# A hybrid block on one core: dumps and chunk loads moved to ScalarE's DMA queue, a third tile for each part of a weight slab, RWKV outputs in the chunks' tiles, transposes in two PSUM banks by turns

## The chip, the cores and the metric

The kernel runs on one core of a Trainium2 chip. A core has five engines with an instruction queue each, and every queue is worked off in its own order: PE (TensorE, matrix products; its weight loads are listed apart as PEld), DVE (VectorE), ACT (ScalarE), POOL (GpSimd) and SP (SyncE, which here does nothing but issue DMAs). ACT can issue DMAs too; it then does so from the same queue in which its activations, copies and casts stand. Data lies in SBUF (128 partitions) or HBM; PE writes to PSUM.

The metric is the device time of one execution in microseconds (us), lower is better.

## The reference, cut to what matters

One transformer block over 512 tokens of width 1024 in float32, with three mixers side by side:

```python
h = rms_norm(x, mix_pre_g[l])
z = h @ w_in[l]                                  # 1024 x 11200
o_hg  = hgrn2_mixer(zq, zf, zi, zog, ...)        # 8 heads, gated linear recurrence
o_rw  = rwkv7_mixer(zrw, ...)                    # 16 heads, state x decay + rank-1 updates
o_mla = mla_mixer(zcq, zckv, zkr, ...)           # 8 heads, causal softmax attention
merged = g_hg*(o_hg @ w_branch[0]) + g_rw*(o_rw @ w_branch[1]) + g_mla*(o_mla @ w_branch[2])
x = x + rms_norm(merged @ w_out[l], mix_post_g[l])
gate, up = split(rms_norm(x, ffn_pre_g[l]) @ w_ffn_in[l])
x = x + rms_norm((silu(gate) * up) @ w_ffn_out[l], ffn_post_g[l])
```

At the end of the RWKV mixer stands, for each token and head, a normalisation over 64 values, an affine (`lnx_g`, `lnx_b`), the sum with a `bonus` and the product with a gate `g`. In the kernel the bonus is kept in HBM as `bv`, the gate as `grw`, and the result as `orw`.

## The kernel before

**Dense streams.** All large products go through `slab` and `stream`. A slab is 256 rows of a weight by 256 columns (256 KB). SP loads it into `wsD` (three buffers), ACT casts it to `whD` (the high part, in PE's reduced float32 type), DVE subtracts to get `wlD` (the low part), and PE makes three products for each tile of it: high by high, high by low, low by high (`mm3`, lines 139 to 141). One slab gives 12 matmuls of 128x512; four slabs fill two PSUM banks `mmD`, which ACT or DVE empties (`zst` for the input projection and the gates, `th` for the branches, `ft` in the FFN). `whD` and `wlD` take the pool's default of two buffers each. In `project` some slabs are held, with as many buffers as are held (`hold`).

**The mixers beside them.** RWKV is prepared in four groups of four heads (`rwkv_group`). Each group fills a tile `G`; its lower-triangular parts go through HBM (`Ld`), are inverted on DVE (`inv`, lines 635 and 636), come back (`Td`) and are merged; then `G` is written to HBM, `rwd`, by four DMAs (lines 460 and 461), two of them of 2240 KB. These are the dumps. After the last group the chain (`rwkv_chain`) runs over eight chunks of 64 tokens; each chunk is loaded by four DMAs of 640 KB from `rwd` (line 682) into one of three buffers `CH`. Their memory is that of `G`, so the first of them has to wait until the last dump has landed. HGRN heads (`ph`, `hq`, `hk`) and the low-rank part of MLA are spread through the same stretch.

**The RWKV tail.** After the chain, for each of eight pieces `p`: four transposes into the PSUM bank `yb` (pool `pY`, one buffer), three activations on ACT into `lno` (two buffers), a load of `bv` into `lnx` (one buffer), an addition on DVE, a load of `grw` into the same `lnx`, a product on DVE, and the store of `orw` (lines 733 to 748). Branch 0 (HGRN's output by its weights) is streamed in the same stretch: its weights, its input `ost` and its gates `th` are loaded by SP as well.

**What sets the order.** The program is written as lanes, each with a priority, and a scheduler with a timeline of its own fixes one order for each engine when the kernel is built; a changed buffer count, queue or tile moves instructions all over the program. At run time each engine follows its list: an instruction that waits holds all that stands behind it. `pace` lets a group of three products start only when the group five before it has ended, through a small memset on POOL (`token`); that is why POOL's list is full of them. DMAs share eight completion semaphores in turn, so a DMA also waits for the one that last had its semaphore.

Of the kernel before, what the change touches and what calls it, by code (L numbers as in the profile page):

```python
# [12 lines left out]
F32R = mybir.dt.float32r  # L13
# [4 lines left out]
ALU = mybir.AluOpType  # L18
# [4 lines left out]
P = 128  # L23
S = 512
# [12 lines left out]
NC = S // C  # L37
# [5 lines left out]
RWC = 5 * P  # L43
# [61 lines left out]
class Kern:  # L105
# [92 lines left out]
    def slab(self, src, pool=None, hold=None):  # L198

        nc = self.nc  # L200
        m, n = src.shape[1:]
        st = self.t(self.wd, [P, m, n], "wsD", bufs=3)
        nc.sync.dma_start(st, src)
        h, l = (self.t(pool or self.wd, [P, m, n], t, F32R, hold) for t in ("whD", "wlD"))
        cur = self.cur_lane
        self.lane(0)
        nc.scalar.copy(h, st)  # L207
        self.split_low(l, st, h)
        self.lane(cur)
        return h, l  # L210
# [231 lines left out]
    def rwkv_group(self, g):  # L442

        all_ = self.t(self.gp, [P, 2, NC, RWC], "G", bufs=2)
        G = self.fields(all_)
        G["all"] = all_
        for e in range(2):

            self.nc.gpsimd.memset(G["PV"][e][e * 64:e * 64 + 64], 0.0)
        G["Ld"] = self.t(self.dpool, [64, 32, 32], "Ld", bufs=2)  # L450
        G["Td"] = self.t(self.dpool, [64, 32, 32], "Td", bufs=2)
        for q in range(2):
            self.lane(5)
            self.rwkv_prep(G, 2 * g + q, q)
        self.lane(3)
        self.rwkv_inverse(G, g)
        self.rwkv_merge(G, g)
        for q in range(2):
            to = self.rwd[g][:, :, q].rearrange("c p n -> p c n")
            self.nc.sync.dma_start(to[:, :NC - 1], all_[:, q, :NC - 1])  # L460
            self.nc.sync.dma_start(to[:, NC - 1, :RWC - P], all_[:, q, NC - 1, :RWC - P])

    def fields(self, t):

# [204 lines left out]
    def rwkv_chain(self):  # L669

        nc, rw = self.nc, self.rw
        V, A, Pl = nc.vector, nc.scalar, nc.gpsimd
        mm = nc.tensor.matmul
        H = [slice(0, 64), slice(64, 128)]
        heads = [(p, e) for p in range(8) for e in range(2)]
        chunks = []

        def load(c):
            t = self.t(rw, [P, 8, RWC], "CH", bufs=3)
            n = RWC if c < NC - 1 else RWC - P  # L680
            for g in range(4):
                nc.sync.dma_start(t[:, 2 * g:2 * g + 2, :n], self.rwd[g][c][:, :, :n])
            chunks.append(self.fields(t))

        load(0)
        St = self.t(rw, [P, 8, C], "St")
        y = self.t(rw, [P, NT, 8, 2, C], "y")
        for c in range(NC):
            if c < NC - 1:
                load(c + 1)  # L690
            G = chunks[c]
            X, PV, LM, BKT = (G[n] for n in ("X", "PV", "LM", "BKT"))
            if 0 < c < NC - 1:

                for e in range(2):
                    Pl.tensor_tensor(St[H[e]], PV[e][H[e]], self.gC[H[e], :, c + 1:c + 2].to_broadcast([64, 8, C]), op=ALU.mult)
            yo = (H[c % 2], H[1 - c % 2])
            z = self.t(self.pC, [P, 8, C], "zus")
            for p, e in heads:
                mm(z[H[e], p, :], lhsT=X[e][:, p, 0:C], rhs=PV[e][:, p, :], start=True, stop=True)  # L700
            zsb = self.t(rw, [P, 8, C], "zsb")
            V.tensor_copy(zsb, z)
            yb = self.t(self.pY, [P, 8, C], "yb")

            self.side_by_side(
                partial(mm, yb[yo[e], p, :], lhsT=X[e][:, p, C:], rhs=PV[e][:, p, :], start=p == 0, stop=False)
                for p, e in heads)
            z = self.t(self.pC, [P, 8, C], "zus")
            for p, e in heads:
                mm(z[H[e], p, :], lhsT=LM[H[e], p, 0:C], rhs=zsb[H[e], p, :], start=True, stop=True)  # L710
            V.tensor_copy(PV[0][H[0]], z[H[0]])
            A.copy(PV[1][H[1]], z[H[1]])
            if c < NC - 1:
                z = self.t(self.pC, [P, 8, C], "zus")
                for p, e in heads:
                    mm(z[H[e], p, :], lhsT=BKT[:, p, H[e]], rhs=PV[e][:, p, :], start=True, stop=True)
                for e in range(2):
                    nxt = chunks[c + 1]["PV"][e][H[e]]
                    if c == 0:
                        V.tensor_copy(nxt, z[H[e]])  # L720
                    else:
                        V.tensor_tensor(nxt, z[H[e]], St[H[e]], op=ALU.add)
            for p, e in heads:
                mm(yb[yo[e], p, :], lhsT=LM[H[e], p, C:], rhs=PV[e][H[e], p, :], start=False, stop=p == 7)
            for e in range(2):
                A.copy(y[yo[e], c // 2, :, e, :], yb[yo[e]])
            if c % 2:
                self.lane(3)
                self.rwkv_norm(y[:, c // 2].rearrange("t p e d -> t (p e) d"))
                self.lane(1)  # L730
        self.lane(3)
        for p in range(8):
            pt = self.t(self.pY, [P, S], "yb")
            for i in range(NT):
                nc.tensor.transpose(pt[:, i * P:(i + 1) * P], y[:, i, p].rearrange("t e d -> t (e d)"), self.ident)
            o = self.t(rw, [P, S], "lno", bufs=2)
            o4 = o.rearrange("f (i j t) -> f i j t", j=2, t=C)
            pt4 = pt.rearrange("f (i j t) -> f i j t", j=2, t=C)
            lb, lg = self.vec("rwkv_lnx_b", p), self.vec("rwkv_lnx_g", p)
            A.activation(o[H[0]], pt[H[0]], AF.Identity, bias=lb[H[0]], scale=lg[H[0]])  # L740
            for j in range(2):

                A.activation(o4[H[1], :, j, :], pt4[H[1], :, 1 - j, :], AF.Identity, bias=lb[H[1]], scale=lg[H[1]])
            for src, op in ((self.bv[p], ALU.add), (self.grw[p], ALU.mult)):
                x = self.t(rw, [P, S], "lnx")
                nc.sync.dma_start(x, src)
                V.tensor_tensor(o, o, x, op=op)  # L747
            nc.sync.dma_start(self.orw[p], o)
            self.dump(f"orw{p}", o)

# [274 lines left out]
    def mla_qv(self):  # L1025
# [8 lines left out]
        def slab(src, kts, nh, n, tag):  # L1034
# [8 lines left out]
            return [[a[:, k].rearrange("p h d -> p (h d)") for k in range(kts)] for a in (h, l)]  # L1043

        w = slab(wq[:, :, :, 128:192], 3, NH, 64, "S")
        self.qr = self.t(self.mv, [P, NH, S], "qr", F32R)
        cs = lambda a, i: a[:, i, :].unsqueeze(1).to_broadcast([P, NH, 32])
# [15 lines left out]
        for hf in range(2):  # L1063
            w = slab(wkv[:, :, 4 * hf:4 * hf + 4, 128:], 2, 4, P, "S")
            for i in range(NT):
                ps = self.t(pM, [P, S], "pm")
                self.dense_tm(ps, w, self.kv, 2, i, slice(0, 512))
                A.copy(self.v[:, i, 4 * hf:4 * hf + 4, :].rearrange("p h d -> p (h d)"), ps)
# [272 lines left out]
```

## Time and profile before

| | us |
|---|---|
| median of 3 runs | 1448.12 (1444.71 to 1449.1) |
| the profiled execution's own time | 1453.48 |
| its span, first to last instruction | 1451.4 |
| PE busy | 1374.8 (95%) |
| DVE busy | 851.0 (59%) |
| ACT busy | 639.3 (44%) |
| mean granted TensorE clock over the span | 0.987 |

The span is what the trace covers; the profiled execution's time is 2.1 us longer. Busy time is the time in which at least one instruction of the engine ran; DMA-issuing instructions do not count as busy. "Idle before" is the time for which an engine stood still just before a group of instructions, with the work that ended most of that time behind an arrow. SP's and ACT's DMA issues are listed as SPq and ACTq.

### The profile page before, as it was taken

The numbers are of one execution on the slowest core, as the hardware profiler recorded it, in microseconds if no ns is written. First come the engines' busy times: TensorE is split into PE (matmuls) and PEld (weight loads), VectorE is DVE, ScalarE is ACT, GpSimd is POOL, SyncE is SP. The second block draws the span as 40 slices with busy tenths as digits, with TensorE's granted clock in tenths as the row PEclk, the third lists the DMA queues.
The fourth block names the chain that finished last, engine by engine and source line by source line (L and its number), as shares of the span: only waits on it lengthen the run. The fifth ranks groups of instructions, "written<-read, shape, count | busy, mean of one in ns | idle before, by whom it ended". The sixth has DMA issues, their size and how long they took to land. (4 is left out here: it accounts for less than half of the span.)

```text
span 1451.4 us, 27450 instructions
## 1 busy us (share of the span) xinstructions
PE 1374.8 (95%) x9664; PEld 1106.8 (76%) x9664; DVE 851.0 (59%) x1756; ACT 639.3 (44%) x1259; POOL 166.0 (11%) x1000
## 2 busy tenths in 40 slices
PE   7999999898999999899998999999999999999997
PEld 6777777666777777778776788887778888888886
DVE  5667876886885785356435646765475443443234
ACT  5564555445554634245354343553354333332222
POOL 3111112111111111123210000000010000000000
PEclk9999999999999999999999999999999999999999
DMA  5555457457548456986367655303545333335323
GB/s 187 153 166 152 146 169 240 151 146 252 153 143 284 131 148 196 398 304 223 96 203 246 196 186 170 90 28 108 193 150 149 98 95 99 98 95 158 97 94 109
DMA packets 186169, 235.82 MB, mean 162 GB/s; under 512 B 33840, under 2 KB 126512, under 8 KB 186032
## 3 DMA queue, kind: packets, MB, share of 16 engines
q1 hardware_dynamic: 184640, 230.91, 50.7%
q10 hardware_dynamic: 1392, 3.15, 0.6%
q8 instruction: 77, 1.26, 0.4%
q14 instruction: 60, 0.49, 0.1%
HBM read 171.75 MB, written 62.26 MB: 161 GB/s over the span
## 5 line engine op out<-in xcount | busy, mean ns | idle before, releaser
L139 PE MATMUL mmD<-xH,whD 128*128 128x512 f32 (+1 forms) x1232 | 490.5, 400 | 29.0 <-ACT whD L207 12.5
L140 PE MATMUL mmD<-xL,whD 128*128 128x512 f32 (+1 forms) x1232 | 476.9, 388 | 0.2 <-DVE xL L134 0.2
L141 PE MATMUL mmD<-xH,wlD 128*128 128x512 f32 (+1 forms) x1232 | 453.4, 390 | 4.1 <-DVE wlD L134 4.1
L134 DVE TENSOR_TENSOR wlD<-wsD,whD 128x512 fp32r<-128x512 f32 x384 | 265.2, 691 | 318.4 <-ACT whD L207 305.7
L207 ACT CAST whD<-wsD 128x512 fp32r<-128x512 f32 x384 | 237.4, 619 | 436.1 <-PE mmD L140 257.9
L139 PEld LDWEIGHTS mmD<-xH,whD 128*128 128x128 f32 x1232 | 234.1, 190 | 84.2 <-issue 24.7
L141 PEld LDWEIGHTS mmD<-xH,wlD 128*128 128x128 f32 x1232 | 232.9, 190 | 56.3 <-DVE wlD L134 8.9
L140 PEld LDWEIGHTS mmD<-xL,whD 128*128 128x128 f32 x1232 | 235.1, 191 | 41.4 <-DVE xL L134 0.5
L151 POOL MEMSET token<- 1x1 f32 x912 | 81.6, 90 | 777.9 <-PE mmD L141 761.7
L140 PE MATMUL po<-wlD,fH 128*128 128x512 f32 x176 | 68.3, 390 | 0.0
L141 PE MATMUL po<-whD,fL 128*128 128x512 f32 x176 | 68.3, 390 | 0.0
L239 ACT COPY zst<-mmD 128x512 f32<-128x512 f32 x64 | 37.5, 586 | 31.3 <-PE mmD L141 31.1
L139 PE MATMUL po<-whD,fH 128*128 128x512 f32 x176 | 50.9, 391 | 0.2
L281 POOL TENSOR_TENSOR rrs<-rtm,mhalf 128x1 f32<-128x1 f32 x8 | 4.7, 589 | 404.6 <-DVE rtm L276 367.5
L635 DVE TENSOR_TENSOR invtmp<-inv 64x30 f32<-64x30 f32 (+14 forms) x120 | 38.5, 320 | 10.5 <-DMA inv<-Ld 8.4
L636 DVE TENSOR_TENSOR inv<-inv,invtmp 64x30 f32<-64x30 f32 (+14 forms) x120 | 38.4, 320 | 2.4
L139 PEld LDWEIGHTS po<-whD,fH 128*128 128x128 f32 x176 | 32.9, 188 | 8.0 <-DVE y L1208 0.6
L141 PEld LDWEIGHTS po<-whD,fL 128*128 128x128 f32 x176 | 33.0, 188 | 7.1
L140 PEld LDWEIGHTS po<-wlD,fH 128*128 128x128 f32 x176 | 33.0, 188 | 7.0
L818 PEld LDWEIGHTS ph<-hq,hk 128*32 128x32 f32 x1536 | 17.0, 113 | 20.1 <-issue 13.4
L747 DVE TENSOR_TENSOR lno<-lno,lnx 128x512 f32<-128x512 f32 x16 | 11.1, 693 | 29.4 <-DMA lnx<-bv 16.4
L1104 ACT ACTIVATE mp<-pm,mmx,scq 128x128 f32<-128x128 f32 (+3 forms) x32 | 19.8, 620 | 16.2 <-DVE mmx L1101 16.1
(344 smaller groups left out, 1962.6 us busy)
## 6 DMA issues: line engine op xcount, KB each, us to landing
wsD<-in_w_in_dram SPq DMA_DIRECT2D x176, 256.0 KB, 3.1
wsD<-in_w_ffn_in_dram SPq DMA_DIRECT2D x96, 256.0 KB, 2.8
rwd<-G SPq DMA_DIRECT2D x8, 2240.0 KB, 11.4
CH<-rwd SPq DMA_DIRECT2D x28, 640.0 KB, 8.1
z<-zst SPq DMA_DIRECT2D x63, 256.0 KB, 2.9
wsD<-in_w_branch_dram SPq DMA_DIRECT2D x48, 256.0 KB, 3.4
wsD<-in_w_ffn_out_dram SPq DMA_DIRECT2D x44, 256.0 KB, 2.6
zr<-z SPq DMA_DIRECT2D x26, 256.0 KB, 3.1
```

What stands on the lines that cost most here:

```text
L134: (eng or self.nc.vector).tensor_tensor(dst, src, high.bitcast(F32), op=ALU.subtract)
L139: first = mm(ps, lhsT=lh, rhs=rh, start=start, stop=False)
L140: mm(ps, lhsT=lh, rhs=rl, start=False, stop=False)
L141: return first, mm(ps, lhsT=ll, rhs=rh, start=False, stop=stop)
L151: token = self.nc.gpsimd.memset(self.token, 0.0).ins
L207: nc.scalar.copy(h, st)
L239: self.nc.scalar.copy(st[:m], ps)
L635: V.tensor_tensor(tv, cv, rv, op=ALU.mult)
L636: V.tensor_tensor(U[:, :j, j + 1:], U[:, :j, j + 1:], tv, op=ALU.add)
L747: V.tensor_tensor(o, o, x, op=op)
L818: mm(g[b:b + HB, o // P, :], lhsT=k[:, t], rhs=q[:, t], start=True, stop=True)
L1104: A.activation(p[:, :n], s_, AF.Exp, bias=mx, scale=self.scq[:, i:i + 1], accum_out=sm)
```

## The change

Four things are changed.

1. `slab`: `whD` and `wlD` get three buffers each wherever no slabs are held (held slabs keep their count).
2. `rwkv_group` and `load` in `rwkv_chain`: the 16 dumps and the 32 chunk loads are issued by ACT and no longer by SP.
3. The RWKV tail: `lno` and `lnx` are gone. Three tiles of the form and name of the chunks' buffers (`CH`) are taken: one for all of `bv`, one for all of `grw`, one for the eight outputs. The 16 loads are issued ahead of the eight pieces.
4. The transposes of the tail go by turns into `yb` (pool `pY`) and `zus` (pool `pC`, free after the chain).

```diff
@@ slab
-        h, l = (self.t(pool or self.wd, [P, m, n], t, F32R, hold) for t in ("whD", "wlD"))
+        h, l = (self.t(pool or self.wd, [P, m, n], t, F32R, hold or 3) for t in ("whD", "wlD"))
@@ rwkv_group
-            self.nc.sync.dma_start(to[:, :NC - 1], all_[:, q, :NC - 1])
-            self.nc.sync.dma_start(to[:, NC - 1, :RWC - P], all_[:, q, NC - 1, :RWC - P])
+
+            self.nc.scalar.dma_start(to[:, :NC - 1], all_[:, q, :NC - 1])
+            self.nc.scalar.dma_start(to[:, NC - 1, :RWC - P], all_[:, q, NC - 1, :RWC - P])
@@ rwkv_chain, load
-                nc.sync.dma_start(t[:, 2 * g:2 * g + 2, :n], self.rwd[g][c][:, :, :n])
+                nc.scalar.dma_start(t[:, 2 * g:2 * g + 2, :n], self.rwd[g][c][:, :, :n])
@@ rwkv_chain, tail
+        bv, gr, out = (self.t(rw, [P, 8, RWC], "CH", bufs=3) for _ in range(3))
         for p in range(8):
-            pt = self.t(self.pY, [P, S], "yb")
+            nc.sync.dma_start(bv[:, p, :S], self.bv[p])
+            nc.sync.dma_start(gr[:, p, :S], self.grw[p])
+        for p in range(8):
+            pt = self.t(self.pC if p % 2 else self.pY, [P, S], "zus" if p % 2 else "yb")
...
-            o = self.t(rw, [P, S], "lno", bufs=2)
+            o = out[:, p, :S]
...
-            for src, op in ((self.bv[p], ALU.add), (self.grw[p], ALU.mult)):
-                x = self.t(rw, [P, S], "lnx")
-                nc.sync.dma_start(x, src)
-                V.tensor_tensor(o, o, x, op=op)
+            V.tensor_tensor(o, o, bv[:, p, :S], op=ALU.add)
+            V.tensor_tensor(o, o, gr[:, p, :S], op=ALU.mult)
```

The built programs have the same matmuls (7578 in both lists of PE); their order differs. Two places are shown, without the numbers at a row's start. In the rows a DMA or an instruction is written as what it writes, an arrow, and what it reads, with the shape; the digits behind a name only tell buffers apart.

**The last dump and the first chunk loads.** Before, they stand in SP's list, between the loads of weight slabs (`wsD`) and the stores of gates (`gth`):

```order
L460 DMA rwd_773_4654<-G_6077 128x7x640
L461 DMA rwd_773_4654<-G_6077 128x512
L460 DMA rwd_773_4654<-G_6077 128x7x640
L461 DMA rwd_773_4654<-G_6077 128x512
L203 DMA wsD_3743<-in_w_in_dram 128x2x256
L254 DMA gth<-zst_3669 128x512
L254 DMA gth<-zst_3672 128x512
L203 DMA wsD_3773<-in_w_in_dram 128x2x256
L203 DMA wsD_3795<-in_w_in_dram 128x2x256
L682 DMA CH_6546<-rwd_770_4651 128x1280
L682 DMA CH_6546<-rwd_771_4652 128x1280
L682 DMA CH_6546<-rwd_772_4653 128x1280
```

Behind the last row SP still has nine loads of the first three chunks, with two gate stores among them, before its next weight slab. In the changed program the chunk loads stand in ACT's list, between casts (`whD`) and the emptying of PSUM banks (`zst`):

```order
L683 DMA CH_6546<-rwd_773_4654 128x1280
L683 DMA CH_6553<-rwd_770_4651 128x1280
L207 CAST whD_3775<-wsD_3773 128x512
L683 DMA CH_6553<-rwd_771_4652 128x1280
L683 DMA CH_6553<-rwd_772_4653 128x1280
L683 DMA CH_6553<-rwd_773_4654 128x1280
L683 DMA CH_6650<-rwd_770_4651 128x1280
L683 DMA CH_6650<-rwd_771_4652 128x1280
L253 ACTIVATE zst_3765<-mmD_3675 128x512
L683 DMA CH_6650<-rwd_772_4653 128x1280
L683 DMA CH_6650<-rwd_773_4654 128x1280
L253 ACTIVATE zst_3768<-mmD_3676 128x512
```

The seven loads behind the cast of `whD_3775` now hold ACT where they held SP; two PSUM banks are emptied only behind them, and the next cast (`whD_3797`) comes after the last row shown.

**The RWKV tail on DVE.** Before, each addition and product of the tail has a cast's subtraction (`wlD`) between it and the next, and each waits for a load into the single `lnx`:

```order
L747 TENSOR_TENSOR lno_7370<-lno_7370,lnx_7374 128x512
L134 TENSOR_TENSOR wlD_4374<-wsD_4371,whD_4373 128x512
L747 TENSOR_TENSOR lno_7370<-lno_7370,lnx_7377 128x512
L134 TENSOR_TENSOR wlD_4396<-wsD_4393,whD_4395 128x512
L134 TENSOR_TENSOR wlD_4418<-wsD_4415,whD_4417 128x512
L747 TENSOR_TENSOR lno_7386<-lno_7386,lnx_7390 128x512
```

Now (`CH_7365` holds `bv`, `CH_7366` holds `grw`, `CH_7367` the outputs):

```order
L750 TENSOR_TENSOR CH_7367<-CH_7367,CH_7365 128x512
L751 TENSOR_TENSOR CH_7367<-CH_7367,CH_7366 128x512
L750 TENSOR_TENSOR CH_7367<-CH_7367,CH_7365 128x512
L134 TENSOR_TENSOR wlD_4470<-wsD_4467,whD_4469 128x512
L751 TENSOR_TENSOR CH_7367<-CH_7367,CH_7366 128x512
L134 TENSOR_TENSOR wlD_4492<-wsD_4489,whD_4491 128x512
L750 TENSOR_TENSOR CH_7367<-CH_7367,CH_7365 128x512
```

The sixteen operations of the tail now stand in a row of some 22 rows on DVE, all before the first input of branch 0 is split, where they were spread over the streams of branch 0 until its first results.

## Prediction

> **What bounds the kernel now.** I read the page first, then a table by stage, then what PE waits for, then the places. All sums below are against the profiled execution: span 1451.4 us and 2.1 us around it, 1453.5 us in all, which is 5.4 us above the median of the three runs (1448.1). I carry every difference over to the median unchanged.
>
> The page's first lines (busy time, share of the span, instructions):
>
> ```profile
> span 1451.4 us, 27450 instructions
> PE 1374.8 (95%) x9664; PEld 1106.8 (76%) x9664; DVE 851.0 (59%) x1756; ACT 639.3 (44%) x1259; POOL 166.0 (11%) x1000
> ```
>
> PE is the bound, and the change leaves its matmuls as they are; so all there is to win or lose lies in 1451.4 - 1374.8 = 76.6 us of PE idle, and in how fast PE's clock runs. The table by stretches (us, PE busy, PEld, DVE, ACT, POOL, granted clock, share of the DMA engines, GB/s) tells where:
>
> ```profile
> 29.00:250.00 221.00, 211.17 (x1558) 164.33 (x1557) 159.75 (x329) 120.08 (x235) 40.34 (x242) 0.99 0.57 171
> 250.00:600.00 350.00, 326.06 (x3096) 249.86 (x3095) 251.75 (x600) 172.82 (x365) 51.75 (x347) 0.97 0.61 191
> 600.00:740.00 140.00, 135.43 (x1653) 110.57 (x1654) 73.23 (x125) 59.62 (x106) 36.43 (x125) 0.99 0.66 229
> 740.00:810.00 70.00, 58.46 (x245) 44.83 (x244) 28.91 (x45) 28.64 (x49) 6.61 (x75) 0.95 0.76 234
> 810.00:1000.00 190.00, 183.51 (x966) 154.35 (x965) 121.37 (x296) 90.30 (x200) 9.60 (x108) 1.00 0.38 117
> 1100.00:1440.00 340.00, 339.44 (x1511) 280.51 (x1510) 135.10 (x206) 105.78 (x182) 1.10 (x2) 1.00 0.35 105
> ```
>
> Between 250 and 600 us (RWKV groups) PE is idle for 23.9 us, in the RWKV tail (740 to 810) for 11.5 us; in the FFN (1100 to 1440) for 0.6 us, so there the third tile can give nothing. The FFN's row also gives PE's pace: 339.44 / 1511 = 0.225 us for a matmul of 128x512, so a slab of 12 is 2.7 us of PE work.
>
> The same view on four short stretches shows the clock:
>
> ```profile
> 352.60:359.40 6.80, 5.41 (x43) 3.96 (x44) 6.22 (x13) 3.21 (x7) 0.32 (x4) 0.50 0.49 150
> 468.60:472.00 3.40, 3.40 (x9) 2.66 (x8) 1.31 (x4) 1.01 (x2) 0.26 (x3) 0.50 0.97 343
> 591.50:594.90 3.40, 3.27 (x22) 2.31 (x23) 1.30 (x3) 1.65 (x6) 0.00 (x0) 0.50 1.05 396
> 799.70:806.50 6.80, 4.60 (x11) 3.66 (x12) 2.49 (x4) 0.00 (x0) 0.18 (x2) 0.50 0.66 213
> ```
>
> In each PE runs at half its clock, in steps of 3.4 us, right behind an idle time (below). A step costs 1.7 us beside the idle time itself.
>
> PE's waits, and one of ACT's, over 200 to 600 us (total, times, longest); the second fence has PE's over the whole span:
>
> ```profile
> PE mmD L139 <- ACT whD L207: 9.3, 7, 3.1
> ACT whD L207 <- DMA wsD<-in_w_in_dram: 21.8, 4, 9.0
> ```
>
> ```profile
> PE mmD L139 <- ACT whD L207: 12.5, 11, 3.1
> PE mmD L139 <- DVE th L1135: 6.1, 3, 4.6
> PE mmD L141 <- DVE wlD L134: 4.1, 7, 1.1
> ```
>
> **Term A, the dumps off SP's queue: -9 us.** SP at the second dump, then ACT and PE (start, duration; in brackets the idle time before):
>
> ```profile
> 334.15 0.37 SPq L460 DMA_DIRECT2D rwd<-G  x1
> 336.36 3.06 SPq L461 DMA_DIRECT2D rwd<-G  x1
> 340.81 1.18 SPq L203 DMA_DIRECT2D wsD<-in_w_in_dram  x1
> 349.73 6.60 SPq L203 DMA_DIRECT2D wsD<-in_w_in_dram  x3
> 353.23 0.62 ACT L207 CAST whD<-wsD 128x512 fp32r<-128x512 f32 x1 [8.96 <-DMA wsD<-in_w_in_dram]
> 353.99 0.76 PE L139 MATMUL mmD<-xH,whD 128*128 128x512 f32 x1 [3.08 <-ACT whD L207]
> ```
>
> Behind the dump a slab's issue takes 1.18 us, and the slabs come so late that ACT stands 8.96 us and PE 3.08, followed by two half-rate steps. This is what the change takes away: SP's queue no longer has the dumps in it. At most it gives the 9.3 us of PE's waits for `whD` in this stretch and four half-rate steps (352.6 to 359.4, 468.6, 591.5), 9.3 + 4 x 1.7 = 16.1 us. It gives nothing if the transfers, not the queue, make the slabs late. A queue's wait of the other kind stays, too, since eight semaphores serve both queues:
>
> ```profile
> SPq L203 <- DMA rwd<-G: 5.3, 3, 3.1
> ```
>
> I take somewhat over half, 9 us: in the row 352.60 the DMA engines are half empty (0.49), so the second dump's stall is the queue's; in the row 591.50, at the last dump, they are full (1.05), and there I expect no gain.
>
> The Trainium skill, "DMA: Bandwidth & Descriptors", section "Issuing engines are not separate DMA queues", says that DMAs started by several engines run on the same 16 DMA engines and that spreading them saves only the issue time. By that rule A is about nothing, which is the second rival below; the 0.49 speaks against it here, the 1.05 for it.
>
> **Term B, the third tile: -3 us.** With three tiles ACT and DVE can be two slabs, 5.4 us of PE work, ahead of the slab in use, where now it is one. PE's waits for `whD` and `wlD` together are 12.5 + 4.1 = 16.6 us; without A's 9.3 some 7 us are left, and 0.6 of them lie in the tail (a row of term C), so 6 us or a little more. The longest for `wlD` is 1.1 us and none for `whD` is over 3.1, so one more slab, 2.7 us, would cover nearly all; but a cast that comes late because ACT or DVE did something else in its list stays late. Bounds 0 and -6; I take the middle.
>
> **Term C, the tail: -9 us.** DVE's additions and PE's first products over 740 to 803 us, by groups (busy, mean ns; idle before), then the worst place:
>
> ```profile
> L747 DVE TENSOR_TENSOR lno<-lno,lnx 128x512 f32<-128x512 f32 x13 | 9.0, 692 | 22.5 <-DMA lnx<-bv 14.8 <-DMA lnx<-grw 7.6
> L139 PE MATMUL mmD<-xH,whD 128*128 128x512 f32 x67 | 27.1, 407 | 9.1 <-DVE th L1135 5.7 <-ACT zst L253 2.3 <-ACT whD L207 0.6
> 796.98 0.69 DVE L747 TENSOR_TENSOR lno<-lno,lnx 128x512 f32<-128x512 f32 x1 [3.96 <-DMA lnx<-bv]
> 801.90 0.77 PE L139 MATMUL mmD<-xH,whD 128*128 128x512 f32 x1 [4.60 <-DVE th L1135]
> ```
>
> DVE stands 22.5 us for the single `lnx`, and behind it in DVE's list stands branch 0's `th`, which frees PE's banks: 4.60 us of PE idle and two half-rate steps (799.7 to 806.5). In the changed order the sixteen operations stand together, their inputs are loaded ahead, and branch 0 comes behind them. Sixteen of 692 ns are 11 us on DVE, which is busy for 28.91 of 70 us, so they lie beside PE's work. At most this gives the stretch's 11.5 us and 3.4 us of clock, 14.9; at least nothing, if the 16 loads of 256 KB in front of the weight slabs make those late in turn. I take the `th` waits (5.7 us) and the two steps (3.4 us), 9 us. What the turn of the two PSUM banks spares is a wait in the same stretch, inside the same bound.
>
> **Term D, what ACT pays: +7 us.** The durations of the issues (min, median, max ns) and SP's own waits in front of the chunk loads (total, times, longest):
>
> ```profile
> L682 SPq DMA_DIRECT2D CH<-rwd x32: 319/426/1586, 590.1 to 670.8; - x32
> L460 SPq DMA_DIRECT2D rwd<-G x8: 367/782/1274, 222.8 to 574.6; - x8
> L461 SPq DMA_DIRECT2D rwd<-G x8: 552/1007/3062, 223.2 to 575.9; - x8
> ...
> SPq L682 <- PE yb L724: 11.8, 5, 4.6
> SPq L682 <- DMA CH<-rwd: 5.1, 5, 1.3
> SPq L682 <- DMA rwd<-G: 2.6, 2, 2.0
> ```
>
> The 48 issues are 32 x 0.43 + 8 x 0.78 + 8 x 1.01 = 28 us of ACT's time, and ACT is busy for under half of it, so as a sum they hide. What can show is ACT standing. A dump's four issues last from 334.15 to 339.42, 5.3 us, which the two slabs ready (5.4 us) just cover: 0 each. The first twelve chunk loads are worse. SP at that place, and ACT and PE:
>
> ```profile
> 590.07 7.48 SPq L682 DMA_DIRECT2D CH<-rwd  x10
> 603.57 0.32 SPq L682 DMA_DIRECT2D CH<-rwd  x1
> 590.86 0.62 ACT L207 CAST whD<-wsD 128x512 fp32r<-128x512 f32 x1 [8.69 <-DMA wsD<-in_w_in_dram]
> 591.62 0.77 PE L139 MATMUL mmD<-xH,whD 128*128 128x512 f32 x1 [2.24 <-ACT whD L207]
> ```
>
> From 590.07 to 603.89 SP is held by them, 13.8 us; PE goes on because ACT still casts and empties banks. In the changed order two banks are emptied and the next slab is cast only behind the last of these loads. If ACT is held as long, PE's cover is the two ready slabs, and 13.8 - 5.4 = 8.4 us are open, of which I take 3 as filled with the first chunk's and HGRN's own matmuls, a choice without a row: about 5, and one half-rate step, 1.7. The later chunks' loads are covered. Bounds: 0, and all of SP's waits at line 682 taken over (11.8 + 5.1 + 2.6 = 19.5 us) with four half-rate steps (6.8), 26.3 us.
>
> **Term E, MLA: -1.5 us.** Two stretches in the heads, with a stream beside them and without:
>
> ```profile
> 870.00:882.00 12.00, 12.00 (x59) 10.04 (x58) 8.76 (x21) 4.85 (x11) 1.06 (x12) 1.00 0.70 205
> 930.42:942.81 12.39, 11.89 (x74) 10.35 (x72) 8.48 (x25) 6.71 (x17) 0.09 (x1) 1.00 0.09 26
> ```
>
> A head alone leaves PE idle for 0.5 us, one beside a stream for none. With the tail done sooner the heads begin sooner: by the two lists of PE, five heads instead of two have input streams between them. Three times 0.5 us.
>
> **The sum.** -9 - 3 - 9 + 7 - 1.5 = -15.5 us: 1453.5 becomes 1438, and the median 1448.1 becomes 1432.6, say 1433. The rest of the program is reordered as well; I know no sign for that, only that places like it cost 1 to 3 us each now.
>
> The Trainium skill, "TensorE: Matmul & The Clock Gate", section "Part 1: The HAM clock gate", has PE fall to half rate after about 3.4 us of idle. By that rule only the 4.60 us at 797 would bring a step; and A without the clock would be some 5 us instead of 9, the sum -11.5 us and the median about 1437. The trace has two steps behind 3.08 us and one behind 2.24 us, so the measurement decides.
>
> **The rivals.**
>
> *The slabs stay late whichever queue the dumps are on.* Both queues feed the same DMA engines, full at 591.5 (1.05). Then A is 0 and the rest stays: -3 - 9 + 7 - 1.5 = -6.5 us, 1442. Against it stands the half-empty 352.6. Chance 0.17.
>
> *ACT stands where SP stood (slower).* The chunk loads' waits move into the queue that casts and empties banks: D is its upper bound, 26.3 us. Then B is nothing, C halves because the chain is late (-4.5), A and E stay: 26.3 - 4.5 - 9 - 1.5 = +11 us, 1459. It decides from the point where D passes the other terms, 22.5 us. For it: SP's 13.8 us. Against it: SP's waits were partly for PE, which ACT has waited for anyway when it copies `y`. Chance 0.19.
>
> *The new order gives back what it wins.* The stalls that no part of the change touches (DVE's list held by other work between 200 and 600 us) fall elsewhere, and D takes some 15 us: within 0.3% (4.3 us) of 1448, which is about what a measurement of this kernel can tell from no change. Chance 0.13.
>
> **How the numbers follow.** My forecast has the remaining 0.51, with a range of its own from 1420 to 1441 (A and C at 13 and 12, or D at 15). Faster by over 0.3%: 0.51 + 0.17 = 0.68, of which 0.01 goes to the middle; same 0.14; slower 0.19. The range for 8 in 10 is 1416 to 1452: below it lie A and C both near their upper bounds (-16.1 - 14.9 with D nearly 0), above it most of the slower rival.
>
> **What would show it.** A: after the change ACT's waits for `wsD` at the first three dumps are under 2 us, and no half-rate step follows them. B: PE's waits for `whD` and `wlD` together are under 8 us. C: 740 to 810 has under 4 us of PE idle, and no step at branch 0's first `th`. D: ACT has 3 to 8 us of waits at the first chunk loads, and PE idle and one step there. E: heads alone are three. I am wrong if PE's idle time behind the chunk loads is over 15 us, if PE still waits for slabs behind the dumps, or if new stalls of several us stand where neither dumps, chunk loads nor the tail are near.

## The result: 1437.4 us after 1447.8 us, and the profile after

The changed kernel takes 1437.4 us (median of 4 runs, 1436.18 to 1439.16) and the kernel before 1447.8 us (4 runs, 1444.71 to 1449.1). The ratio is 0.9932, with a 95% interval from 0.9912 to 0.9953: about 10 us faster. The profiled execution of the change took 1436.18 us, 1.2 us below its median, while that of before (1453.48 us) lay 5.7 us above its own. The two traces therefore differ by 17 us, and 7 of them are only the choice of the execution.

The first lines of the page after, with PE's idle time of 1434.4 - 1364.7 = 69.7 us (76.6 before):

```profile
span 1434.4 us, 27281 instructions
PE 1364.7 (95%) x9664; PEld 1106.5 (77%) x9664; DVE 853.0 (59%) x1756; ACT 637.4 (44%) x1259; POOL 166.4 (12%) x1000
```

The table by stretches of the kernel after (us, PE busy, PEld, DVE, ACT, POOL, granted clock, share of the DMA engines, GB/s):

```profile
29.00:250.00 221.00, 206.00 (x1533) 160.11 (x1534) 157.39 (x324) 115.71 (x219) 37.76 (x239) 0.99 0.56 169
250.00:600.00 350.00, 323.83 (x2932) 250.88 (x2933) 245.70 (x581) 169.26 (x358) 52.73 (x351) 0.98 0.63 201
600.00:740.00 140.00, 138.25 (x1851) 113.44 (x1847) 83.65 (x150) 63.24 (x124) 38.37 (x125) 0.99 0.68 230
740.00:810.00 70.00, 69.09 (x329) 56.89 (x328) 43.74 (x79) 41.89 (x73) 6.09 (x69) 1.00 0.63 197
```

The RWKV tail (740 to 810) has 0.9 us of PE idle where it had 11.5, and its clock is whole. The two stretches ahead of it, with the RWKV groups, the dumps and the first chunk loads, are worse than before: 15.0 us in place of 9.8, and 26.2 in place of 23.9. So the win of the tail is partly spent there, and not by the moved DMAs alone. In the first stretch PE's idle time rises by 3.4 us at the first dump (215 to 250 us: 0.3 to 3.7 us), but also by 3.6 us between 100 and 150 us, where no dump stands (1.0 to 4.6 us). `no_queue` below has the latter too (4.5 us), `two_tiles` does not (0.9): it comes with the order that the third tile brings.

PE's waits over the whole span, after (total, times, longest):

```profile
PE mmD L139 <- ACT zst L239: 6.3, 5, 2.8
PE pr L550 <- ACT t L548: 6.2, 4, 2.9
PE mmD L139 <- ACT zst L253: 4.4, 2, 3.5
PE mmD L139 <- ACT whD L207: 4.2, 1, 4.2
PE mmD L141 <- DVE wlD L134: 1.4, 3, 0.8
```

The waits for slabs (`whD`, 12.5 us before) have become one. The waits for PSUM banks that ACT empties late (`zst`) have grown from 3.8 and 2.3 us to 6.3 and 4.4, and those for `t`, an input of the next RWKV group that ACT computes, are new. The longest of line 239 stands right behind the first dump. ACT and then PE at that place (start, duration; in brackets the idle time before):

```profile
225.60 0.40 ACTq L461 DMA_DIRECT2D rwd<-G  x1
226.03 0.58 ACTq L462 DMA_DIRECT2D rwd<-G  x1
226.78 1.03 ACTq L461 DMA_DIRECT2D rwd<-G  x1
227.84 3.66 ACTq L462 DMA_DIRECT2D rwd<-G  x1
233.43 0.58 ACT L239 COPY zst<-mmD 128x512 f32<-128x512 f32 x1
```

```profile
234.16 0.66 PE L139 MATMUL mmD<-xH,whD 128*128 128x512 f32 x1 [2.82 <-ACT zst L239]
```

ACT issues the four DMAs of the dump from 225.60 to 231.50, 5.9 us. The casts are covered by the third tile, but the emptying of a bank stands behind the dump in ACT's list, and PE stands 2.82 us for it. The third dump shows the same with an activation of the next group's preparation (`t`, 2.87 us), and both are followed by a step of half clock:

```profile
480.15 0.69 PE L550 MATMUL pr<-cst,t 128*128 128x128 f32 x2 [2.87 <-ACT t L548]
```

```profile
234.30:237.70 3.40, 3.40 (x9) 2.53 (x9) 3.34 (x7) 1.60 (x4) 0.18 (x2) 0.50 1.04 415
480.00:483.40 3.40, 3.25 (x9) 2.54 (x10) 2.08 (x5) 2.07 (x5) 0.09 (x1) 0.51 1.04 407
579.00:585.80 6.80, 4.59 (x11) 3.65 (x12) 1.99 (x3) 1.76 (x3) 0.26 (x3) 0.50 0.77 278
592.70:596.10 3.40, 2.87 (x8) 1.88 (x8) 0.07 (x1) 1.96 (x5) 0.09 (x1) 0.50 1.03 401
```

The last two rows lie at the first chunk loads. There ACT is held once more, by five loads in one piece (ACT, then PE):

```profile
582.16 10.23 ACTq L683 DMA_DIRECT2D CH<-rwd  x5
592.49 0.60 ACT L253 ACTIVATE zst<-mmD 128x512 f32<-128x512 f32 x1 [9.74 <-DMA CH<-rwd]
```

```profile
581.21 0.77 PE L139 MATMUL mmD<-xH,whD 128*128 128x512 f32 x1 [4.22 <-ACT whD L207]
593.24 0.77 PE L139 MATMUL mmD<-xH,whD 128*128 128x512 f32 x1 [3.53 <-ACT zst L253]
```

7.75 us of idle time and three steps of 1.7 us, 12.9 us in all, against 2.24 + 1.7 at this place before.

### The profile page after: what moved, and what is told of

Read it like the earlier page. It is cut to its first block, busy times and chain, and to the rows that moved or that the text cites. A ratio compares the mean times of both kernels' runs of the same rounds, so it can differ in the third digit from the quotient of the medians.

```text
span 1434.4 us, 27281 instructions
## 1 busy us (share of the span) xinstructions
PE 1364.7 (95%) x9664; PEld 1106.5 (77%) x9664; DVE 853.0 (59%) x1756; ACT 637.4 (44%) x1259; POOL 166.4 (12%) x1000
## 3 DMA queue, kind: packets, MB, share of 16 engines
q10 hardware_dynamic: 14960, 44.05, 8.3%
## 4 chain that ended last, share of the span: by engine, by line
PE 75%; DMA 9%; DVE 6%; ACT 4%; issue 3%; ACTq 1%; SPq 1%; POOL 0%; DVEq 0%; POOLq 0%
PE mmD L139 17%; PE mmD L140 16%; PE mmD L141 16%; PE po L140 4%; PE po L141 4%; PE po L139 4%; DMA z<-zst 1%; DMA hz<-z 1%; DMA rwd<-G 1%; DMA zr<-z 1%; PE pm L139 1%; PE pm L140 1%; PE pm L141 1%; PE pr L196 1%; PE pmo L1117 1%
## 5 line engine op out<-in xcount | busy, mean ns | idle before, releaser
L141 PE MATMUL mmD<-xH,wlD 128*128 128x512 f32 (+1 forms) x1232 | 471.7, 387 | 1.5 <-DVE wlD L134 1.4
L139 PE MATMUL po<-whD,fH 128*128 128x512 f32 x176 | 62.0, 390 | 0.0
L239 ACT COPY zst<-mmD 128x512 f32<-128x512 f32 x64 | 37.4, 584 | 15.8 <-PE mmD L141 15.5
L1115 ACT COPY mpT<-pmt 128x128 f32<-128x128 f32 (+3 forms) x32 | 13.6, 425 | 29.2 <-PE pmt L1113 28.9
L1117 PEld LDWEIGHTS pmo<-mpT,mv 128*128 128x128 f32 x160 | 22.3, 191 | 4.7 <-ACT mpT L1115 2.6
## 6 DMA issues: line engine op xcount, KB each, us to landing
rwd<-G ACTq DMA_DIRECT2D x8, 2240.0 KB, 11.6
```

The lines of the kernel that those rows point to most:

```text
L139: first = mm(ps, lhsT=lh, rhs=rh, start=start, stop=False)
L141: return first, mm(ps, lhsT=ll, rhs=rh, start=False, stop=stop)
L239: self.nc.scalar.copy(st[:m], ps)
L1117: mm(pq[:, t], lhsT=self.v[:, j, h, :], rhs=pT[:, j * P:(j + 1) * P], start=j == 0, stop=j == i)
```

## The experiments

Every ratio is to the kernel before, run on the same chip in the same session (9 to 11 runs of it, medians 1445.9 to 1446.9; the change's own ratio is that of the result); a thousandth is 1.45 us. The intervals are some 0.002 to each side, so a difference of two ratios is uncertain by about 0.003, or 4 us.

### Which part of the change pays

`no_queue` is the change with dumps and chunk loads back on SP, `two_tiles` the change with two tiles for each part of a slab. `tail_only` is the kernel before with the new tail, `queue_only` the kernel before with dumps and chunk loads on ACT. A third tile with the old tail was not tried: memory does not hold both, since it is the tail's use of the chunks' buffers that frees the room.

```diff
@@ no_queue (against the change); queue_only is the reverse against the kernel before
-            self.nc.scalar.dma_start(to[:, :NC - 1], all_[:, q, :NC - 1])
+            self.nc.sync.dma_start(to[:, :NC - 1], all_[:, q, :NC - 1])
...
-                nc.scalar.dma_start(t[:, 2 * g:2 * g + 2, :n], self.rwd[g][c][:, :, :n])
+                nc.sync.dma_start(t[:, 2 * g:2 * g + 2, :n], self.rwd[g][c][:, :, :n])
@@ two_tiles (against the change)
-        h, l = (self.t(pool or self.wd, [P, m, n], t, F32R, hold or 3) for t in ("whD", "wlD"))
+        h, l = (self.t(pool or self.wd, [P, m, n], t, F32R, hold) for t in ("whD", "wlD"))
```

Expected of `no_queue`:

> The changed kernel with dumps and chunk loads back on SP's queue; third tile and new tail stay. Theory 1 (the queue part costs as much as it gives or more, because a dump's issues and the chunk loads hold ACT: in the changed kernel's trace PE idles 2.82, 1.71, 2.87, 4.22 and 3.53 us behind them, with some five half-rate steps of 1.7 us): without it those 23 us go, and the stalls that the dumps made on SP's queue before, 3.08, 1.4 and 2.24 us with four steps, come back less what the third tile covers; about 1430, between 1426 and 1437. Theory 2 (as predicted, the queue part gives 9 and costs 7 us): 1438 to 1442. Theory 3 (the differences are the new order's, not the part's): anything within 6 us of 1437.

Expected of `tail_only`:

> The kernel before with the new tail alone (bv, grw and the outputs in chunk tiles, two banks by turns); two tiles for each part, everything on SP. Theory 1 and theory 2: the tail alone gives the 11 us of PE idle between 740 and 810 us and the two half-rate steps at 799.7, so 1434 to 1439, that is, all of the measured gain. Theory 3: within 6 us of 1448 or 1437 without a relation to the tail; the stretch behind the chain would not show the gain.

Expected of `queue_only`:

> The kernel before with dumps and chunk loads on ACT's queue alone; two tiles, old tail. Theory 1: slower than before or the same, since ACT's holds are not covered by a third tile: 1448 to 1460. Theory 2: 9 less 7 us, 1443 to 1450, with no stall behind the first three dumps.

Expected of `two_tiles`:

> The changed kernel with two tiles for each part of a slab instead of three; queue and new tail stay. Theory 1: with ACT held for 4 to 6 us at each dump and for 14 us at the first chunk loads, one ready slab instead of two lets PE idle 2.7 us more at five places: 10 to 14 us slower than the changed kernel, 1447 to 1452. Theory 2 (the third tile gives 3 us): 1440 to 1442.

| | tail | third tile | queue | median, us | ratio, 95% interval |
|---|---|---|---|---|---|
| tail_only | new | no | SP | 1428.5 | 0.9880 (0.9863 to 0.9898) |
| no_queue | new | yes | SP | 1426.2 | 0.9869 (0.9848 to 0.9891) |
| two_tiles | new | no | ACT | 1437.6 | 0.9936 (0.9919 to 0.9952) |
| the change | new | yes | ACT | 1437.4 | 0.9932 (0.9912 to 0.9953) |
| queue_only | old | no | ACT | 1456.8 | 1.0076 (1.0059 to 1.0093) |

The queue was measured three times and costs each time: +11 us with the old tail (1.0076), +8 with the new tail (0.9936 against 0.9880), +9 with tail and tiles (0.9932 against 0.9869). The tail alone gives 17 us (interval 15 to 20). The third tile gives 0.6 or 1.6 us, which cannot be told from nothing. It does what it was meant for: from `tail_only` to `no_queue` PE's waits for `whD` and `wlD` fall from 15.9 to 1.9 us. But PE's whole idle time falls from 60.9 to 57.9 us only, since other waits grow in the new order (for POOL's `token` from 2.6 to 5.9 us, for ACT's `t` from 0.2 to 2.5).

The tail in `tail_only`, whose list of PE in the trace is that of before up to 621 us:

```profile
740.00:810.00 70.00, 68.91 (x322) 56.42 (x321) 38.36 (x71) 38.92 (x68) 5.64 (x64) 1.00 0.57 178
810.00:1000.00 190.00, 186.12 (x969) 157.07 (x968) 120.62 (x284) 84.71 (x187) 13.24 (x148) 1.00 0.44 138
```

Idle time falls from 11.5 to 1.1 us in the tail and from 6.5 to 3.9 behind it, 13.0 us, and the two half-rate steps at 799.7 (3.4 us) are gone. That makes 16.4 us, beside the 17 us of the ratio; the two traced executions as a whole differ by 21.

### Which DMAs cost on ACT: the dumps or the chunk loads

`loads_sp` is the change with the 32 chunk loads on SP, `dumps_sp` the change with the 16 dumps on SP, each by the one or the other half of the diff above.

> The changed kernel with the 32 chunk loads issued by SP again; the 16 dumps stay on ACT. The part of the change that moves DMAs to ACT's queue costs 9 to 11 us; the question is which DMAs. Theory 1 (the chunk loads): at the first loads the changed kernel's trace has 4.22 and 3.53 us of PE idle and three half-rate steps (5.1 us), 12.9 us, against 2.24 and 1.7 at that place before; with the loads on SP these 9 us come back: about 1428 us. Theory 2 (the dumps): the three places behind dumps stay as they are (2.82 + 1.7, 1.71, 2.87 + 1.7 us) and nothing is won: 1435 to 1438. Theory 3 (both, half each): about 1432.

> The changed kernel with the 16 dumps issued by SP again; the 32 chunk loads stay on ACT. Theory 1 (the chunk loads cost, the dumps on ACT cost nothing): 1435 to 1438, as the changed kernel. Theory 2 (the dumps on ACT cost): the three stalls behind them go, some 10 us, less what SP's own hold behind dumps gives back: about 1428. Theory 3 (half each): about 1432. If the prediction's step A were real (dumps off SP's queue win 9 us) and only the loads cost, this kernel would be slower than the changed one: about 1446.

Measured: `loads_sp` 1430.5 us (0.9900, 0.9877 to 0.9923), `dumps_sp` 1431.7 us (0.9893, 0.9870 to 0.9916). By the ratios, taking the loads back gives 4.6 us, taking the dumps back 5.6 us, and both together (`no_queue`) 9.1 us. Theory 3 of these texts, half each, fits; each half alone is hardly beyond its uncertainty, so the places have to bear it out, and they do. In `loads_sp` the stall behind the first dump stays:

```profile
235.25 0.47 PE L139 MATMUL mmD<-xH,whD 128*128 128x512 f32 x1 [2.96 <-ACT zst L239]
```

In `dumps_sp` it is gone, and the place of the first chunk loads is nearly as bad as in the change, with 6.98 us of PE idle and two steps (ACT, then PE):

```profile
574.19 10.28 ACTq L683 DMA_DIRECT2D CH<-rwd  x5
584.57 0.60 ACT L253 ACTIVATE zst<-mmD 128x512 f32<-128x512 f32 x1 [10.01 <-DMA CH<-rwd]
```

```profile
585.31 0.77 PE L139 MATMUL mmD<-xH,whD 128*128 128x512 f32 x1 [6.04 <-ACT zst L253]
```

### Is it the number of chunk loads

`one_load_act` keeps all four groups in one tensor in HBM and loads a chunk by one DMA of 2560 KB in place of four of 640 KB; `one_load_sp` does the same with dumps and loads on SP.

```diff
@@ one_load_act (against the change)
-        self.rwd = [self.t(self.dpool, [NC, P, 2, RWC], f"rwd{g}") for g in range(4)]
+        self.rwd = self.t(self.dpool, [NC, P, 8, RWC], "rwd")
...
-            for g in range(4):
-                nc.scalar.dma_start(t[:, 2 * g:2 * g + 2, :n], self.rwd[g][c][:, :, :n])
+            nc.scalar.dma_start(t[:, :, :n], self.rwd[c][:, :, :n])
```

> The changed kernel with one tensor in HBM for all four groups, so that a chunk is loaded by one DMA of 2560 KB and not by four of 640 KB; issuing engines stay as in the changed kernel (ACT). The same bytes move. Theory 1 (ACT's hold at the first twelve loads comes from their number: each waits in turn for an earlier load to land): three issues in place of twelve, the hold of 9.7 us and PE's 3.53 us behind it with two half-rate steps go, about 1430. Theory 2 (the transfer itself makes slabs and banks late): as the changed kernel, 1435 to 1438. Theory 3: a DMA of 2560 KB takes ACT four times as long to issue, and the hold stays or grows: 1437 to 1442.

> The same single load for each chunk, and dumps and loads both issued by SP (the kernel with tail and third tile alone, 1426 us in its run, with one DMA for each chunk). If SP's hold at the first twelve loads (13.8 us in the kernel before) still made slabs late there, it wins 2 to 5 us: 1421 to 1424. If with three tiles that hold is covered already: 1425 to 1428. If the larger DMAs push weight slabs aside: 1429 or more.

Measured: `one_load_act` 1434.7 us (0.9921, 0.9900 to 0.9943), 1.6 us under the change and not to be told from it; `one_load_sp` 1430.6 us (0.9895, 0.9872 to 0.9919), 3.8 us over `no_queue`, which is within the uncertainty too. The hold of ACT did go: the first loads take 0.81 and 0.37 us, and casts follow at once. But PE then stands later, at a step of the chain:

```profile
579.33 0.81 ACTq L682 DMA_DIRECT2D CH<-rwd  x2
580.25 0.37 ACTq L682 DMA_DIRECT2D CH<-rwd  x1
```

```profile
619.24 1.97 PE L710 MATMUL zus<-zsb,CH 64*64 64x64 f32 x32 [4.31 <-DVE zsb L702]
```

So the hold went with the number of loads, as theory 1 has it, and its removal was given back; `one_load_sp` has the same stall (4.62 us). The single issues of the change bear theory 1 out: the last four of the five loads that stand in one piece there (below) take ACT 0.33 us each, but begin 2 to 3.5 us apart, each within 0.02 us of the landing of the earlier load that had its semaphore. This hold is a wait for landings, and the profile names it (`DMA CH<-rwd`, 9.74 us).

```profile
583.48 0.33 ACTq L683 DMA_DIRECT2D CH<-rwd  x1
586.99 0.33 ACTq L683 DMA_DIRECT2D CH<-rwd  x1
590.11 0.33 ACTq L683 DMA_DIRECT2D CH<-rwd  x1
592.06 0.33 ACTq L683 DMA_DIRECT2D CH<-rwd  x1
```

The order of the program changes with the number of DMAs, so whether that stall comes from the larger loads or from the order is open.

### What holds ACT at a dump

In the change the narrow layout of `rwd` (chunk by chunk) makes a dump write seven pieces of 2.5 KB for each partition. `wide_act` lays the groups out by partition, so that these are 17.5 KB in a row. The lists of PE, DVE, POOL and SP are the change's, and ACT's is too but for the shape of its DMAs. The layout works the other way on the chunk loads: one piece of 5 KB for each partition becomes two of 2.5 KB. `wide_sp` stands to `no_queue` in the same way.

```diff
@@ wide_act (against the change), wide_sp (against no_queue)
-        self.rwd = [self.t(self.dpool, [NC, P, 2, RWC], f"rwd{g}") for g in range(4)]
+        self.rwd = [self.t(self.dpool, [P, 2, NC, RWC], f"rwd{g}") for g in range(4)]
...
-            to = self.rwd[g][:, :, q].rearrange("c p n -> p c n")
+            to = self.rwd[g][:, q]
...
-                nc.scalar.dma_start(t[:, 2 * g:2 * g + 2, :n], self.rwd[g][c][:, :, :n])
+                nc.scalar.dma_start(t[:, 2 * g:2 * g + 2, :n], self.rwd[g][:, :, c, :n])
```

> The changed kernel with another layout of the dumped groups in HBM: per partition, not per chunk, so that a dump of 2240 KB writes 17.5 KB in a row for each partition in place of seven pieces of 2.5 KB. Every engine's list of instructions is the changed kernel's; dumps and chunk loads stay on ACT and move the same bytes. The changed kernel holds ACT for 5.9 us at the first dump (225.60 to 231.50, the last issue 3.66 us), and PE then stands 2.82 us there and 2.87 us at the third dump, each with a half-rate step. Theory 1 (the hold is the number of pieces that the issue has to queue): the long issue falls under 1.5 us, the two stalls and their steps go, 5 to 9 us: 1429 to 1432. Theory 2 (the hold is a wait for DMAs under way, by bytes or by the shared semaphores): the issues stay at 3 to 4 us and the time at 1435 to 1438.

> The same layout with dumps and chunk loads on SP (tail and third tile of the change, 1426 us in its run). If SP's hold behind the dumps still makes slabs late, it wins up to 5 us: 1421 to 1424. If the third tile covers it already: 1425 to 1428. If the wider pieces take the DMA engines longer away from the weight slabs: 1429 or more.

Measured: `wide_act` 1422.7 us (0.9845, 0.9829 to 0.9861), 12.6 us under the change by the ratios; `wide_sp` 1426.6 us (0.9875, 0.9849 to 0.9900), as `no_queue`. The issues of the dumps (min, median, max ns) in the change and in `wide_act`:

```profile
L461 ACTq DMA_DIRECT2D rwd<-G x8: 377/715/1205, 225.6 to 561.2; - x8
L462 ACTq DMA_DIRECT2D rwd<-G x8: 472/1990/4419, 226.0 to 562.3; - x8
```

```profile
L461 ACTq DMA_DIRECT2D rwd<-G x8: 326/584/897, 226.8 to 548.6; - x8
L462 ACTq DMA_DIRECT2D rwd<-G x8: 342/831/1296, 227.1 to 549.4; - x8
```

The longest issue falls from 4.42 to 1.30 us, and in `wide_act` PE has no idle time over 0.3 us in the 10 us behind the first and the third dump. Theory 1 holds, and its price was set too low (5 to 9 us): the hold of ACT at the dumps costs 12.6 us. On SP, where the longest issue falls from 3.20 us (`no_queue`) to 1.26 (`wide_sp`), no price can be told from nothing.

Since PE's lists are the same, one instruction can be followed through both traces. `wide_act` gains 4.3 us on the change at the first dump, 4.1 at the second, 4.7 at the third and nothing at the fourth, 13.1 us in all, and is 13.4 us ahead at the end. So the gain lies at the dumps.

The packets of ACT's queue fell from 14960 to 12400 at equal bytes (the page's part on queues), and the long DMA of a dump still takes 11.2 us from issue to landing (median), 11.6 in the change; in this pair the issue shrank, and the transfer hardly.

### What the chunk loads still cost

In `wide_act` the first loads hold ACT even longer (ACT, then PE):

```profile
567.86 11.54 ACTq L683 DMA_DIRECT2D CH<-rwd  x5
579.50 0.60 ACT L253 ACTIVATE zst<-mmD 128x512 f32<-128x512 f32 x1 [11.04 <-DMA CH<-rwd]
```

```profile
580.24 0.76 PE L139 MATMUL mmD<-xH,whD 128*128 128x512 f32 x1 [7.41 <-ACT zst L253]
```

`wide_loads_sp` has the wide dumps on ACT and the chunk loads on SP; `wide_one_act` has wide dumps on ACT and one load for each chunk on ACT. Their edits are those shown above.

> The dumps in wide pieces on ACT, the chunk loads on SP: the dumps' half of the queue change without the loads' half. In the run with wide dumps and loads both on ACT (1422.7 us) the first loads still hold ACT for 11.54 us, and PE stands 1.99 and 7.41 us there with three half-rate steps, 14.5 us in all. Theory 1 (prices add): that place costs about 4 us with the loads on SP, as in the kernel before (2.24 + 1.7): 1411 to 1415. Theory 2 (the loads' price was 5 us in the narrow layout, and what is won at one place is lost half elsewhere): 1416 to 1419. Theory 3 (wide pieces were the whole gain, the place of the loads no longer matters): 1421 to 1424.

> Wide dumps on ACT, and each chunk loaded by one DMA of 2560 KB on ACT. In the narrow layout the single load took PE's 3.53 us behind the first loads away, but PE then stood 4.3 us at a later step of the chain, and the time fell by 1.5 to 3 us only. Theory 1 (the place is worth 14.5 us with wide dumps, and most of it goes): 1411 to 1416. Theory 2 (as in the narrow layout, most comes back in the chain): 1418 to 1422.

Measured: `wide_loads_sp` 1418.2 us (0.9811, 0.9798 to 0.9825), `wide_one_act` 1419.4 us (0.9823, 0.9809 to 0.9836). Theory 2 of both texts: the place was worth 14.5 us in the trace, and by the ratios 4.9 and 3.2 us of them reach the end. Against `loads_sp`, whose lists of PE, DVE and POOL it shares, `wide_loads_sp` is 12.9 us faster. That is a second measurement of the dumps' hold, but not a clean one: by PE's instructions in the two traces 8.4 us are gained up to the first chunk loads, and 4.4 behind them, where `loads_sp` has a wait of 3.81 us for a slab and three half-rate steps. With the loads on SP, SP is held instead, for 12.11 us, and PE pays 2.24 us, as in the kernel before but without a step (SP, then PE):

```profile
566.60 12.11 SPq L683 DMA_DIRECT2D CH<-rwd  x12
```

```profile
592.41 0.47 PE L139 MATMUL mmD<-xH,whD 128*128 128x512 f32 x1 [2.24 <-ACT whD L207]
```

In `wide_one_act` the third load alone holds ACT (below). Its issue, in eight pieces of 2.5 KB for each partition and behind two such loads of 0.60 and 0.68 us, lasts 5.35 us; the third of `one_load_act`, 20 KB in a row, took 0.37. So a long issue behind others in many pieces is seen at the loads too.

```profile
567.78 5.35 ACTq L682 DMA_DIRECT2D CH<-rwd  x1
```

`wide_loads_sp` is the fastest version: 27 us under the kernel before by its ratio, 17 us under the change.

## Why the prediction was right in its number, and where it was not

The forecast was 1433 us (1420 to 1441 as its own range), the result 1437.4. The sum was -15.5 us and the medians moved by -10.4. Two parts of it were off by more than that difference, in opposite directions: D was some 10 us too small (17.4 against 7), C and E together 7 us (17.4 against 10.5). That the sum came out so near is in part luck.

**Term D failed, at "0 each" for the dumps.** That step compared a dump's four issues (5.3 us on SP) with two ready slabs (5.4 us) and found them covered. The casts are covered, but ACT does more than cast: it empties PE's banks (`zst`) and computes the next group's inputs (`t`), and for these no third tile exists. The price of the hold is 12.6 us by the ratio of `wide_act`, against 0 in the sum; in the traces 13.1 us of gain lie at the dumps there, and 8.4 in the other pair with the same lists. For the chunk loads D took 5 + 1.7 = 6.7 us; measured were 4.6 us (narrow) and 4.9 (wide). The mechanism there was right (banks emptied behind the loads, half-rate steps), but the sign was missed in size: ACT waits 9.7 us where 3 to 8 were forecast, and the trace has three steps where one was.

**Term A, the dumps off SP's queue, -9.** Its argument rests on a row read at the wrong place. The half-empty DMA engines (0.49) are those of 352.6 to 359.4 us, when the late slabs had come. Between the dump's last issue and that of the last late slab the engines were full in the kernel before (us, PE busy, PEld, DVE, ACT, POOL, granted clock, share of the DMA engines, GB/s):

```profile
336.40:349.70 13.30, 12.65 (x149) 9.49 (x148) 9.36 (x20) 6.66 (x11) 2.81 (x15) 1.00 1.02 359
```

So the row gave no ground against the rival that blames the transfers. The runs do: between 200 and 600 us the waits of ACT's casts for slabs are 21.8 us before and 22.1 in `tail_only`, and with the dumps on ACT and still two tiles (`queue_only`, `two_tiles`) the view has none, though the engines are as full (0.98 at 343 to 360 us, at the second dump of `queue_only`). So the slabs were late by SP's queue, as A has it, as far as two pairs can show it whose order differs too.

What it is worth is less clear. With the hold left in, moving the dumps costs 4.5 to 5.6 us. With it taken out, the same move (`wide_sp` against `wide_loads_sp`, loads on SP in both) gives 0.9875 to 0.9811, 9.3 us, uncertain by 4. So the size of A may well have been right; -9.3 + 12.6 + 4.8 makes +8.1 us, and the whole queue part measured +8 to +11. But that pair differs in the order of all engines, and PE's waits for late slabs, which A priced, are not seen in it. PE's waits for `whD` between 200 and 600 us (total, times, longest), in `no_queue` and then in `wide_loads_sp`:

```profile
PE mmD L139 <- ACT whD L207: 1.6, 2, 1.2
```

```profile
PE mmD L139 <- ACT whD L207: 3.0, 2, 2.2
```

Before they were 9.3 us. With the third tile they are small even where the dumps stay on SP (in `wide_sp` the view has none), so the lateness that A priced is covered by the tile. The first lines of `wide_sp` and then of `wide_loads_sp`:

```profile
span 1423.6 us, 27292 instructions
PE 1364.1 (96%) x9664; PEld 1107.6 (78%) x9664; DVE 850.5 (60%) x1756; ACT 639.9 (45%) x1259; POOL 167.7 (12%) x1000
```

```profile
span 1416.6 us, 27281 instructions
PE 1357.2 (96%) x9664; PEld 1104.5 (78%) x9664; DVE 853.2 (60%) x1756; ACT 638.4 (45%) x1259; POOL 165.9 (12%) x1000
```

PE's idle time is the same, 59.5 and 59.4 us; its busy time, with the same matmuls, differs by 6.9. About half of that is the clock: it is at half for 26.1 us of the first span and 19.3 of the second. One of the steps that only `wide_sp` has (469.0) follows a wait of 2.46 us for POOL's `token`, not for a slab. The rest of these 9 us is open. Of its two signs, ACT's waits for slabs between 200 and 600 us fell, from 21.8 to 7.7 us in the change; half-rate steps behind the dumps did not go, they changed their cause.

**Term C, the tail, -9, and E, the heads, -1.5, were undersized.** Together they measured -17.4 us (-14.7 to -19.8). The bound of C, 14.9 us, counted the stretch from 740 to 810 us alone; PE's idle time behind it fell as well (6.5 to 3.9 us), where E had 1.5. And C's value was taken too low within its bound: 10.4 of the 11.5 us of idle time went, not only the 5.7 for `th`. The signs held: 0.9 us of idle time in that stretch, no step, and three heads without a stream beside them.

**Term B, the third tile, -3**: 0.6 and 1.6 us, inside its bounds of 0 and -6 and not to be told from 0. Its sign, waits for `whD` and `wlD` under 8 us, held (4.2 + 1.4), and shows how little a sign says on time: the waits that went were replaced by those for `zst`, `t` and `token`.

**The rivals.** *The slabs stay late whichever queue* (1442; it is the first of the three, though term A calls it the second) is not what happened: the slabs came in time, as `queue_only` shows, and ACT stood. *The new order gives back* is not needed. *ACT stands where SP stood* named the right mechanism: ACT's hold sums to some 12.6 + 4.8 = 17.4 us, under the 22.5 us from which it decides; it stood for the larger part at the dumps, where neither the forecast nor this rival had put it.

The Trainium skill, "DMA: Bandwidth & Descriptors", section "Issuing engines are not separate DMA queues", says that issuing from several engines saves only sequencer time, which is usually small beside the DMA itself. The runs agree that ACT's queue made the dumps no faster: the median from issue to landing of their long DMAs was 11.4 us on SP before and 11.6 on ACT. But the time to issue was not small here: 5.9 us for a dump's four issues, and it falls on whichever engine issues.

## What to carry to other kernels

Before DMAs are moved to a computing engine's queue, list everything that stands behind them in that engine's list, and not only the instruction whose wait is to be cured: here the casts were covered, and the emptying of banks behind the same issue was not. Long issues are a price of the DMA's shape; a destination that is contiguous for each partition cut them from 4.4 to 1.3 us here, and the fastest version has the dumps on ACT in that form. Many DMAs issued one behind the other hold the engine as well, until earlier ones land. And measure the parts of a change one by one: this one was 10 us faster as a sum of -17, about -1 and about +9.

## What was not expected of the hardware

- The time that an issue holds its engine depends on how many pieces the DMAs have: 4.42 us at the longest for a 256 KB DMA behind one of 2240 KB in pieces of 2.5 KB, 1.30 us when the larger one wrote 17.5 KB in a row. On SP the kernel's time did not change with it measurably, on ACT by 12.6 us.
- ACT stood 9.74 us in a row of loads whose issues take 0.33 us each: each began when an earlier load had landed.
- Half-rate steps follow idle times of 2.82 and 2.87 us here, as they followed 3.08 and 2.24 us before. Not each such idle time brings one: the clock stayed whole behind 2.80 us in `loads_sp` (479.45) and 2.24 us in `wide_loads_sp` (592.41). The Trainium skill, "TensorE: Matmul & The Clock Gate", section "Part 1: The HAM clock gate", gives a window of some 3.4 us that runs freely; the steps last about that long (3.40 us), but these idle times in front of them were shorter than it.
- A chunk's load by one DMA of 2560 KB was no faster than by four of 640 KB (0.9921 against 0.9932 on ACT, 0.9895 against 0.9869 on SP), though ACT's hold of 9.74 us went; the order of the program differs too, so this is no clean measurement of the DMA.
